# First stage of a decoder block: another order of loads, norms, rotary tables and latent projections

## The chip, the cores and the metric

One core of a Trainium2 chip runs the whole kernel. The time is the device time of one execution in microseconds (us); lower is better. The engines are TensorE (PE; its weight loads are listed apart as PEld), VectorE (DVE), ScalarE (ACT), GpSimd (POOL) and SyncE (SP), which here only issues transfers (DMA).

## What is computed

The reference is one decoder layer on x of 512 rows by 1024 columns, in float32:

```python
h = rmsnorm(x, g_mix)
z = h @ w_in      # [pool channels 512 | q latent 256 | kv latent 128 | rotary key 64 | gate A | gate B]
u_pool, c_q, c_kv, k_rope_in, gate_a, gate_b = split(z)
a  = pool_mixer(u_pool, ...)                 # windows 2/4/8/16, per-group maps
bm = mla_mixer(c_q, c_kv, k_rope_in, cos, sin, ...)   # norms of the latents, 8 heads, causal softmax
x = x + (sigmoid(gate_a) * a + sigmoid(gate_b) * bm) @ w_out
x = x + relu(rmsnorm(x, g_mlp) @ w_mlp_in)**2 @ w_mlp_out
out = rmsnorm(x, g_final)
```

cos and sin come from positions times inverse frequencies.

## The kernel before

Every float32 product is made of three passes on TensorE: an operand is split into a high part (a copy rounded to a narrower format, written by ScalarE) and a low part (operand minus high part, by VectorE), and high x high, low x high and high x low are added up in one PSUM bank. In the first stage the passes are called HH (high row, high weight), LH (low row, high weight) and HL (high row, low weight).

The first stage is what stands ahead of the gates. x comes as four tiles of 128 rows (`xs[0..3]`). For tile t, `square(t)` sums its squares on ScalarE and forms the reciprocal root (a small add on VectorE, a power on GpSimd), `scale_rows` multiplies the row by it and by the broadcast gain `g_bc` (two halves on VectorE, tile `n1h`), and `transpose_rows` turns it on TensorE through PSUM tiles `n1pt` (eight 128x128 transposes in two halves) and splits it into `h_hi` and `h_lo`.

The latent projection multiplies each tile by 448 columns of `w_in` (q latent, kv latent, rotary key). Its weights come as four chunks `C[0]` to `C[3]` of two row blocks each: `lat_hi(c)` casts a chunk's high part on ScalarE (`whi`), `lat_lo(c, engine)` makes its low part (`wlo`) on the engine named. `latents_mm(t, chunks, passes)` issues the matmuls, 24 for a tile, into that tile's PSUM tile `lat`. `latents_end(t)` norms the latents and turns the rotary key by the tables; `latents_t(t)` transposes the finished row `lrow` through PSUM tiles `lpt` and splits it.

The rotary tables (`ck`, `sk` and scaled copies) are made by a generator, `rotary_tables()`: some 15 small instructions on VectorE and two sines on ScalarE; each `next(rot)` issues a step of it. Then come the four pooling projections: `load_u(g)` loads and splits their weights, `pool_in(g)` does 24 matmuls of 512 columns into a PSUM tile `u`. The `lat` and `u` tiles share one pool of four banks (`psM`), so `u0` takes the bank of `lat` tile 0 and must wait until its last reader is done. Four raw buffers and four high and low buffers are shared by all weight chunks in turn.

Nothing is scheduled by cost here: all engines run their instructions in the order in which the code of this stage writes them (manual schedule), each engine for itself, and wait on each other by semaphores. SP issues the loads in the order written; eight can be on their way at a time, the ninth waits for the first. TensorE is kept busy at the start by `NWARM` matmuls on zeros (`warm`).

Of the kernel before, what the change touches and what calls it, by code (L numbers as in the profile page):

```python
# [11 lines left out]
F32 = mybir.dt.float32  # L12
# [7 lines left out]
P = 128  # L20
# [15 lines left out]
C_Q = PW  # L36
C_GA = PW + QL + KVL + DR
C_GB = C_GA + D
LAT = QL + KVL + DR
FFG = 8  # L40
NWARM = 4

COST = {"A": (0.165, 0.00083), "V": (0.155, 0.00104)}
UP_US, DOWN_US = 2.86, 2.78
# [4 lines left out]
def block_kernel(ctx: ExitStack, tc: tile.TileContext, x, positions, g_mix, w_in, b_gate,  # L49
                 pool_w, pool_scale, w_pool_proj, g_q, w_uq, g_kv, w_ukv, w_attn_proj,  # L50
                 w_out, g_mlp, w_mlp_in, w_mlp_out, g_final, inv_freq, inv_count, out):
    nc = tc.nc
# [43 lines left out]
    def load_chunk(srcs, cols, parts=False, own=None):  # L96

        n = nchunk[0]
        nchunk[0] += 1
        raw = wp.tile([P, 1024], F32, name=f"raw{n}", tag=f"raw{n % 4}", bufs=1)  # L100
        hi = (own or wp).tile([P, 1024], F32R, name=f"whi{n}", tag="whi", bufs=4)
        lo = (own or wp).tile([P, 1024], F32R, name=f"wlo{n}", tag="wlo", bufs=4)
        for view, src in srcs:
            nc.sync.dma_start(view(raw), src)
        if parts:
            return raw, hi, lo
        split(raw[:, :cols], hi[:, :cols], lo[:, :cols])
        return hi, lo
# [6 lines left out]
    w_in_v = w_in.rearrange("(k p) c -> p k c", p=P)  # L115
# [129 lines left out]
    with ExitStack() as pre:  # L245
# [14 lines left out]
        gl_bc = tb.tile([P, QL + KVL], F32, name="gl_bc")  # L260
        icnt = tb.tile([P, 16], F32, name="icnt")
        vrow = tb.tile([20, P], F32, name="vrow")
        nc.sync.dma_start(xs[0], x_v[0])
        nc.sync.dma_start(pos_i, positions.rearrange("(t p) -> p t", p=P))
        nc.sync.dma_start(frq, inv_freq.partition_broadcast(P))
        nc.sync.dma_start(g_bc, g_mix.partition_broadcast(P))
        nc.sync.dma_start(xs[1], x_v[1])
        lv = lambda t: t[:, :2 * LAT].rearrange("p (a b) -> p a b", a=2)
        lraw = [load_chunk([(lv, w_in_v[:, 2 * c:2 * c + 2, C_Q:C_Q + LAT])], 2 * LAT, True) for c in range(4)]
        lw = [(lv(hi), lv(lo)) for _, hi, lo in lraw]  # L270
        for t in (2, 3):
            nc.sync.dma_start(xs[t], x_v[t])
        nc.sync.dma_start(gl_bc[:, :QL], g_q.partition_broadcast(P))
        nc.sync.dma_start(gl_bc[:, QL:], g_kv.partition_broadcast(P))
        nc.sync.dma_start(vrow[:2 * KD, :], b_gate.rearrange("(k p) -> k p", p=P))
# [64 lines left out]
        lat_ps = {}  # L340

        def latents_mm(t, ks, passes):
# [5 lines left out]
            for k in ks:  # L348
                whi, wlo = lw[k // 2]
                for p in passes:  # L350
# [2 lines left out]
                    nc.tensor.matmul(ps[:, :LAT], h[:, k, tok], w[:, k % 2, :], start=len(done) == 1,  # L353
                                     stop=len(done) == 3 * KD)

        def latents_end(t):
            ps = lat_ps.pop(t)[0]
            junk = tmp1.tile([P, QL], F32, name=f"ljunk{t}", tag="ljunk", bufs=1)
            ms = small.tile([P, 2], F32, name=f"lms{t}", tag="lms")
            nc.scalar.activation(junk, ps[:, :QL], AF.Square, scale=1.0 / math.sqrt(QL), accum_out=ms[:, 0:1])  # L360
            nc.scalar.activation(junk[:, :KVL], ps[:, QL:QL + KVL], AF.Square,
                                 scale=1.0 / math.sqrt(KVL), accum_out=ms[:, 1:2])
            r = rstd_of(ms, 2, "l")
            row = tmp1.tile([P, 4, P], F32, name=f"lrow{t}", tag="lrow")
# [25 lines left out]
        def square(t):  # L390
            junk = tmp.tile([P, D], F32, name=f"n1junk{t}", tag="junk", bufs=1)
            ms = small.tile([P, 1], F32, name=f"n1ms{t}", tag="n1ms")
            nc.scalar.activation(junk, xs[t], AF.Square, scale=1.0 / math.sqrt(D), accum_out=ms)
            return rstd_of(ms, 1, "n1")

        def scale_rows(t, r):
            h = tmp.tile([P, D], F32, name=f"n1h{t}", tag="hrow")
            for c in range(2):
                cs = slice(c * 512, (c + 1) * 512)
                nc.vector.scalar_tensor_tensor(out=h[:, cs], in0=xs[t][:, cs], scalar=r, in1=g_bc[:, cs],  # L400
                                               op0=ALU.mult, op1=ALU.mult)
            return h

        def lat_hi(c):
            raw, hi, _ = lraw[c]
            nc.scalar.copy(hi[:, :2 * LAT], raw[:, :2 * LAT])

        def lat_lo(c, eng):
            raw, hi, lo = (t[:, :2 * LAT] for t in lraw[c])
            eng.tensor_tensor(out=lo, in0=raw, in1=f32(hi), op=ALU.subtract)  # L410


        def load_u(g):
            W["u", g] = chunk(w_in_v[:, :, g * P:(g + 1) * P], KD, P)
# [99 lines left out]
        rot = rotary_tables()  # L514
        C = [(2 * c, 2 * c + 1) for c in range(4)]
        HH, LH, HL = (0,), (1,), (2,)
        next(rot)
        r0 = square(0)
        next(rot)
        h0 = scale_rows(0, r0)  # L520
        r1 = square(1)
        next(rot)
        transpose_rows(h0, 0, h_hi, h_lo, psT, "n1")
        next(rot)
        lat_hi(0)
        latents_mm(0, C[0], HH)
        h1 = scale_rows(1, r1)
        lat_lo(0, nc.vector)
        lat_hi(1)
        lat_lo(1, nc.gpsimd)  # L530
        latents_mm(0, C[0], LH)
        latents_mm(0, C[1], HH)
        lat_hi(2)
        transpose_rows(h1, 1, h_hi, h_lo, psT, "n1")
        latents_mm(0, C[1], LH)
        latents_mm(0, C[0], HL)
        lat_hi(3)
        lat_lo(3, nc.gpsimd)
        lat_lo(2, nc.vector)
        latents_mm(0, C[2], HH + LH)  # L540
        latents_mm(1, C[0] + C[1], HH)
        latents_mm(0, C[1], HL)
        r2 = square(2)
        latents_mm(1, C[0], LH + HL)
        latents_mm(0, C[3], HH + LH)
        latents_mm(0, C[2], HL)
        next(rot)
        r3 = square(3)
        h2 = scale_rows(2, r2)
        latents_mm(0, C[3], HL)  # L550
        latents_mm(1, C[1], LH + HL)
        next(rot)
        transpose_rows(h2, 2, h_hi, h_lo, psT, "n1")
        h3 = scale_rows(3, r3)
        for _ in rot:
            pass
        latents_mm(1, C[2] + C[3], HH + LH + HL)
        latents_end(0)
        transpose_rows(h3, 3, h_hi, h_lo, psT, "n1")
        latents_mm(2, C[0] + C[1], HH + LH + HL)  # L560
        latents_end(1)
        latents_mm(2, C[2] + C[3], HH + LH + HL)
        latents_t(0)
        latents_mm(3, C[0] + C[1], HH + LH + HL)
        load_u(0)
        latents_end(2)
        latents_t(1)
        latents_mm(3, C[2] + C[3], HH + LH + HL)
        load_u(1)
        latents_end(3)  # L570
        pv = psT.tile([P, 20], F32, name="pv", tag="T")
        nc.tensor.transpose(pv, vrow, ident[:20, :20])
        nc.vector.tensor_copy(vec, pv)
        nrm.close()
        tmp2 = pool(mixer, "tmp2", bufs=2)
        pool_in(0)
        latents_t(2)
        nc.sync.dma_start(praw, pool_w.rearrange("g c d -> c g d"))
        load_u(2)
        pool_in(1)  # L580
        latents_t(3)
        pool_diff(0)
        load_u(3)
        pool_in(2)
        pool_diff(1)
        load_a(0)
# [898 lines left out]
```

## Time and profile before

| | |
|---|---|
| median of three runs | 684.94 us (684.65 to 686.38) |
| the profiled execution | 685.97 us, of which its span 684.2 us |
| mean granted TensorE clock | 0.991 of full speed (2.4 GHz) |
| TensorE busy | 663.0 us (97%) |
| VectorE, ScalarE, GpSimd busy | 516.0, 376.5, 83.2 us |

The span runs from the first to the last instruction of the program. A busy share over the whole span hides stages with different limits; the first 20 us look unlike the rest. The granted clock is the share of full speed that TensorE was given in a stretch: 1.00 is 2.4 GHz and 0.50 is 1.2 GHz; before the first recorded change it reads 1.00.

### The profile page before, as it was taken

The numbers are of one execution on the slowest core, as the hardware profiler recorded it, in microseconds if no ns is written. First come the engines' busy times: TensorE is split into PE (matmuls) and PEld (weight loads), VectorE is DVE, ScalarE is ACT, GpSimd is POOL, SyncE is SP. The second block draws the span as 40 slices with busy tenths as digits, with TensorE's granted clock in tenths as the row PEclk, the third lists the DMA queues.
The fourth block names the chain that finished last, engine by engine and source line by source line (L and its number), as shares of the span: only waits on it lengthen the run. The fifth ranks groups of instructions, "written<-read, shape, count | busy, mean of one in ns | idle before, by whom it ended". The sixth has DMA issues, their size and how long they took to land.

```text
span 684.2 us, 9775 instructions
## 1 busy us (share of the span) xinstructions
PE 663.0 (97%) x3681; PEld 570.0 (83%) x3681; DVE 516.0 (75%) x793; ACT 376.5 (55%) x613; POOL 83.2 (12%) x101
## 2 busy tenths in 40 slices
PE   6999999999999999999998999999999999999994
PEld 3888888888888888888888977899889988899883
DVE  5767852478788764564579989788987989799996
ACT  4545252446655544442267784488535874368735
POOL 2216600000000000000000212002200022001212
PEclk8999999999999999999999999999999999999998
DMA  7423354642221125747504679338973398444953
GB/s 274 139 62 94 95 152 129 174 128 63 69 69 47 47 93 186 224 130 233 166 0 125 174 170 238 96 123 183 215 188 122 95 215 174 135 154 140 231 92 124
DMA packets 87047, 95.24 MB, mean 139 GB/s; under 512 B 6468, under 2 KB 61528, under 8 KB 87000
## 3 DMA queue, kind: packets, MB, share of 16 engines
q1 hardware_dynamic: 78296, 77.84, 36.1%
q0 software_dynamic: 8704, 16.78, 14.5%
q8 instruction: 29, 0.48, 0.3%
q14 instruction: 18, 0.15, 0.1%
HBM read 88.31 MB, written 6.29 MB: 138 GB/s over the span
## 4 chain that ended last, share of the span: by engine, by line
PE 89%; DVE 5%; ACT 2%; issue 1%; DMA 1%; POOL 0%; SPq 0%; POOLq 0%; DVEq 0%; ACTq 0%
PE P L777 7%; PE P L778 7%; PE P L776 7%; PE b L826 6%; PE a L826 5%; PE c L826 3%; PE v L826 3%; PE u L421 3%; PE lat L353 3%; PE e L826 2%; PE wo L777 2%; PE ga L71 2%; PE gb L70 2%; PE ga L70 2%; PE wo L776 2%; PE ga L72 2%
## 5 line engine op out<-in xcount | busy, mean ns | idle before, releaser
L929 ACT CAST xhi<-r_X 128x1024 fp32r<-128x1024 f32 x84 | 88.1, 1051 | 68.8 <-PE P L778 25.7
L932 DVE TENSOR_TENSOR xlo<-r_X,xhi 128x1024 fp32r<-128x1024 f32 x84 | 102.5, 1222 | 20.8 <-ACT xhi L929 20.3
L777 PE MATMUL P<-xlo,rhi 128*128 128x512 f32 (+1 forms) x228 | 89.5, 392 | 1.6 <-DVE xlo L932 1.5
L778 PE MATMUL P<-xhi,rlo 128*128 128x512 f32 (+1 forms) x228 | 89.1, 391 | 0.0
L776 PE MATMUL P<-xhi,rhi 128*128 128x512 f32 (+1 forms) x228 | 89.1, 391 | 0.0
L65 ACT CAST whi<-raw 128x1024 fp32r<-128x1024 f32 x45 | 46.7, 1050 | 45.4 <-PE bm L71 17.2
L66 DVE TENSOR_TENSOR wlo<-raw,whi 128x1024 fp32r<-128x1024 f32 x45 | 55.3, 1234 | 18.7 <-ACT whi L65 17.5
L777 PEld LDWEIGHTS P<-xlo,rhi 128*128 128x128 f32 x228 | 42.7, 187 | 12.7 <-DVE xlo L932 2.9
L776 PEld LDWEIGHTS P<-xhi,rhi 128*128 128x128 f32 x228 | 42.7, 187 | 10.0
L778 PEld LDWEIGHTS P<-xhi,rlo 128*128 128x128 f32 x228 | 42.7, 187 | 10.0
L915 POOL DMA_DIRECT2D r_X<-in_w_mlp_out x24 | 29.1, 1210 | 120.9 <-DVE xlo L932 116.6
L940 DVE TENSOR_TENSOR r_X<-r_X,r_X 128x1024 f32<-128x1024 f32 x32 | 39.1, 1223 | 5.0 <-DMA r_X<-in_w_mlp_in 4.5
L1081 DVE TENSOR_TENSOR rlo<-F,rhi 128x512 fp32r<-128x512 f32 x56 | 37.6, 687 | 6.9 <-ACT rhi L1078 6.8
L1078 ACT CAST rhi<-F 128x512 fp32r<-128x512 f32 x56 | 33.3, 620 | 1.0 <-DVE F L1087 0.5
L1122 DVE TENSOR_TENSOR xa<-xa,P 128x512 f32<-128x512 f32 (+1 forms) x53 | 33.0, 672 | 0.7 <-PE P L778 0.7
L665 ACT ACTIVATE p<-s,nm 128x128 f32<-128x128 f32 (+3 forms) x32 | 16.9, 528 | 19.9 <-DVE nm L662 19.4
L915 POOL DMA_DIRECT2D r_T<-in_w_mlp_out x8 | 9.7, 1213 | 145.3 <-ACT rhi L1078 49.5
L826 PE MATMUL a<-mb_hi,xhi 128*128 128x256 f32 x96 | 27.0, 281 | 0.0
L826 PE MATMUL a<-mb_hi,xlo 128*128 128x256 f32 x96 | 27.0, 281 | 0.0
L826 PE MATMUL a<-mb_lo,xhi 128*128 128x256 f32 x96 | 27.0, 281 | 0.0
L70 PE MATMUL gb<-h_hi,whi 128*128 128x512 f32 x64 | 26.4, 412 | 0.0
L71 PE MATMUL gb<-h_lo,whi 128*128 128x512 f32 x64 | 25.6, 400 | 0.0
(297 smaller groups left out, 1923.9 us busy)
## 6 DMA issues: line engine op xcount, KB each, us to landing
r_X<-in_w_mlp_in SPq DMA_DIRECT2D x32, 512.0 KB, 4.6
r_X<-in_w_mlp_out POOLq DMA_DIRECT2D x24, 512.0 KB, 6.5
raw<-in_w_in SPq DMA_DIRECT2D x20, 512.0 KB, 4.0
r<-in_w_mlp_out SPq DMA_DIRECT2D x16, 512.0 KB, 6.2
raw<-in_w_attn_proj SPq DMA_DIRECT2D x8, 512.0 KB, 3.5
raw<-in_w_out SPq DMA_DIRECT2D x8, 512.0 KB, 4.9
r_X<-in_w_mlp_out SPq DMA_DIRECT2D x8, 512.0 KB, 4.0
r_T<-in_w_mlp_out SPq DMA_DIRECT2D x8, 512.0 KB, 4.0
```

Source lines behind the costliest of these rows:

```text
L65: nc.scalar.copy(hi, src)
L66: (lo_eng or nc.vector).tensor_tensor(out=lo, in0=src, in1=f32(hi), op=ALU.subtract)
L70: nc.tensor.matmul(acc, whi, ahi, start=first, stop=False)
L71: nc.tensor.matmul(acc, whi, alo, start=False, stop=False)
L776: nc.tensor.matmul(acc, a_hi, w_hi, start=first, stop=False, skip_group_check=again)
L777: nc.tensor.matmul(acc, a_hi, w_lo, start=False, stop=False, skip_group_check=again)
L778: nc.tensor.matmul(acc, a_lo, w_hi, start=False, stop=last, skip_group_check=again)
L826: nc.tensor.matmul(acc[:, j, :], u[:, k, js], b[:, k, :], start=fresh and j + k + n == 0, stop=j == 1 and k == 3 and n == 2, skip_group_ch ...
L915: op = Op("G", ADD_US, lambda: nc.gpsimd.dma_start(buf.tile.rearrange("p (a b) -> p a b", a=a), src, accum_op=ALU.add), needs, rank_now[0])
L929: nc.scalar.copy(hi, buf.tile)
L932: lo_op = use(vec_op(1024, lambda: nc.vector.tensor_tensor(out=pb.tile[1], in0=buf.tile, in1=f32(pb.tile[0]), op=SUB), [hi_op], k), buf)
L940: return use(vec_op(1024, lambda: nc.vector.tensor_tensor(out=O.tile, in0=A.tile, in1=Bb.tile, op=op), needs, rank_now[0]), *{A, Bb, O})
```

## The change

The loads are issued in another order; the steps of the rotary tables move behind the fourth tile's scaling; all four low parts of the latent weights are made on VectorE; `latents_end` is cut in two, so that the second half (`latents_row`) is issued one tile later, with four row buffers instead of two; the latent transposes move behind the first two pooling projections; the matmuls of the latent projection come in another order; and there are three warm-up matmuls instead of four.

```diff
-NWARM = 4
+NWARM = 3
...
         nc.sync.dma_start(xs[0], x_v[0])
+        nc.sync.dma_start(g_bc, g_mix.partition_broadcast(P))
+        load_lat(0)
+        nc.sync.dma_start(xs[1], x_v[1])
+        for c in (1, 2):
+            load_lat(c)
+        nc.sync.dma_start(xs[2], x_v[2])
+        load_lat(3)
+        lw = [(lv(hi), lv(lo)) for _, hi, lo in lraw]
+        nc.sync.dma_start(xs[3], x_v[3])
         nc.sync.dma_start(pos_i, positions.rearrange("(t p) -> p t", p=P))
         nc.sync.dma_start(frq, inv_freq.partition_broadcast(P))
-        nc.sync.dma_start(g_bc, g_mix.partition_broadcast(P))
-        nc.sync.dma_start(xs[1], x_v[1])
...
-            r = rstd_of(ms, 2, "l")
-            row = tmp1.tile([P, 4, P], F32, name=f"lrow{t}", tag="lrow")
+            lat_r[t] = rstd_of(ms, 2, "l")
+
+        def latents_row(t):
+            ps, r = lat_ps.pop(t)[0], lat_r.pop(t)
+            row = tmp1.tile([P, 4, P], F32, name=f"lrow{t}", tag="lrow", bufs=4)
...
-        next(rot)
         r0 = square(0)
-        next(rot)
         h0 = scale_rows(0, r0)
+        lat_hi(0)
+        transpose_rows(h0, 0, h_hi, h_lo, psT, "n1")
         r1 = square(1)
-        next(rot)
-        transpose_rows(h0, 0, h_hi, h_lo, psT, "n1")
-        next(rot)
-        lat_hi(0)
-        latents_mm(0, C[0], HH)
+        latents_mm(0, C[0], HH + LH)
+        lat_hi(1)
         h1 = scale_rows(1, r1)
         lat_lo(0, nc.vector)
-        lat_hi(1)
-        lat_lo(1, nc.gpsimd)
...
-        lat_lo(3, nc.gpsimd)
...
+        latents_mm(1, C[2], HH + LH)
         transpose_rows(h2, 2, h_hi, h_lo, psT, "n1")
+        lat_lo(3, nc.vector)
+        for t in range(2):
+            latents_mm(t, C[2], HL)
+            latents_mm(t, C[3], HH + LH)
         h3 = scale_rows(3, r3)
+        for _ in range(4):
+            next(rot)
+        for t in range(2):
+            latents_mm(t, C[3], HL)
+        latents_mm(2, C[0], HH + LH + HL)
+        transpose_rows(h3, 3, h_hi, h_lo, psT, "n1")
         for _ in rot:
             pass
...
         latents_end(1)
-        latents_mm(2, C[2] + C[3], HH + LH + HL)
-        latents_t(0)
-        latents_mm(3, C[0] + C[1], HH + LH + HL)
+        latents_row(0)
+        latents_mm(3, C[0], HH + LH + HL)
         load_u(0)
...
         pool_in(0)
+        latents_t(0)
+        latents_t(1)
+        load_u(3)
+        nc.sync.dma_start(praw, pool_w.rearrange("g c d -> c g d"))
+        pool_in(1)
         latents_t(2)
```

SP's queue at the start of the program, before; `x_115` to `x_118` are the four x tiles, `raw_...` with 2x448 the latent weight chunks, `pos_i` and `frq` positions and frequencies:

```order
L263 DMA x_115<-in_x 128x1024
L264 DMA pos_i<-in_positions 128x4x1
L265 DMA frq<-inv_freq 128x32
L266 DMA g_bc<-in_g_mix 128x1024
L267 DMA x_116<-in_x 128x1024
L104 DMA raw_128<-in_w_in 128x2x448
L104 DMA raw_132<-in_w_in 128x2x448
```

and now:

```order
L269 DMA x_115<-in_x 128x1024
L270 DMA g_bc<-in_g_mix 128x1024
L104 DMA raw_125<-in_w_in 128x2x448
L272 DMA x_116<-in_x 128x1024
L104 DMA raw_130<-in_w_in 128x2x448
L104 DMA raw_134<-in_w_in 128x2x448
L275 DMA x_117<-in_x 128x1024
L104 DMA raw_139<-in_w_in 128x2x448
L278 DMA x_118<-in_x 128x1024
L279 DMA pos_i<-in_positions 128x4x1
L280 DMA frq<-inv_freq 128x32
```

Positions and frequencies moved from the second and third place to behind the last x tile, and the first weight chunk to ahead of the second x tile.

VectorE from its fourth instruction on, before; `n1v` is the small add of a norm, `ang` and `kk` belong to the rotary tables:

```order
L293 CAST pos_f<-pos_i 128x4
L296 TENSOR_SCALAR ang<-frq,pos_f 128x32 x4
L88 TENSOR_SCALAR n1v<-n1ms_186 128x1
L314 TENSOR_SCALAR kk<-ang 128x128
L316 TENSOR_SCALAR kk<-kk 128x128
L400 SCALAR_TENSOR_TENSOR n1h_195<-x_115,n1r,g_bc 128x512 x2
L88 TENSOR_SCALAR n1v<-n1ms_199 128x1
L319 SCALAR_TENSOR_TENSOR ang<-kk,ang 128x128 x2
L66 TENSOR_TENSOR h_lo<-n1pt_0_207,h_hi 128x4x128
```

and now:

```order
L88 TENSOR_SCALAR n1v<-n1ms_178 128x1
L413 SCALAR_TENSOR_TENSOR n1h_184<-x_115,n1r,g_bc 128x512 x2
L66 TENSOR_TENSOR h_lo<-n1pt_0_188,h_hi 128x4x128
L66 TENSOR_TENSOR h_lo<-n1pt_1_195,h_hi 128x4x128
L88 TENSOR_SCALAR n1v<-n1ms_203 128x1
L413 SCALAR_TENSOR_TENSOR n1h_215<-x_116,n1r,g_bc 128x512 x2
L423 TENSOR_TENSOR wlo_127<-raw_125,whi_126 128x896
L66 TENSOR_TENSOR h_lo<-n1pt_0_224,h_hi 128x4x128
```

The table instructions no longer stand among the norms; the norm's add comes first.

TensorE's first rows, before; `lat_224` is the first tile's projection, `n1pt_0` and `n1pt_1` the two halves of a tile's transposes:

```order
L513 MATMUL warm<-wz 128x512 x4
L143 MATMUL n1pt_0_207<-ident,n1h_195 128x128 x4
L143 MATMUL n1pt_1_214<-ident,n1h_195 128x128 x4
L353 MATMUL lat_224<-whi_129,h_hi 128x448 x2
L353 MATMUL lat_224<-whi_129,h_lo 128x448 x2
L353 MATMUL lat_224<-whi_133,h_hi 128x448 x2
L143 MATMUL n1pt_0_238<-ident,n1h_227 128x128 x4
```

and now:

```order
L526 MATMUL warm<-wz 128x512 x3
L143 MATMUL n1pt_0_188<-ident,n1h_184 128x128 x4
L143 MATMUL n1pt_1_195<-ident,n1h_184 128x128 x4
L361 MATMUL lat_209<-whi_126,h_hi 128x448
L361 MATMUL lat_209<-whi_126,h_lo 128x448
L361 MATMUL lat_209<-whi_126,h_hi 128x448
L361 MATMUL lat_209<-whi_126,h_lo 128x448
L361 MATMUL lat_209<-whi_131,h_hi 128x448
```

A high and a low row now alternate, and four matmuls on the second chunk, not two, stand ahead of the second tile's transposes.

## Rows read from the trace of the kernel before

**Rows 1.** The page: TensorE's busy tenths in 40 slices of the span.

```profile
PE   6999999999999999999998999999999999999994
```

**Rows 2.** Windows: length, busy us of each engine, granted clock, DMA share, GB/s.

```profile
7.00:13.40 6.40, 2.54 (x13) 1.34 (x12) 4.15 (x13) 3.54 (x6) 1.11 (x2) 1.00 1.04 401
13.40:20.30 6.90, 6.00 (x21) 5.02 (x20) 6.51 (x7) 4.09 (x7) 3.24 (x2) 0.51 0.58 192
20.30:52.50 32.20, 32.16 (x165) 27.66 (x164) 22.08 (x66) 14.20 (x40) 6.83 (x9) 1.00 0.35 97
...
53.00:350.00 297.00, 297.00 (x1447) 247.04 (x1447) 192.47 (x353) 138.67 (x263) 27.56 (x41) 1.00 0.40 121
```

**Rows 3.** Chain that ended last, in order of time: start, us, what.

```profile
2.66 7.11 DMA x<-in_x
9.86 1.16 ACT n1junk L393 x2
...
13.37 3.26 DVE n1h L400 x2
...
25.13 0.87 PE n1pt L143 x8
...
29.61 4.96 PE lat L353 x24
...
46.27 0.44 PE lpt L385 x4
46.71 5.60 PE u L421 x24
```

**Rows 4.** Windows of the first loads; the last column is GB/s.

```profile
3.00:5.50 2.50, 2.50 (x4) 1.01 (x3) 0.17 (x1) 1.15 (x2) 0.00 (x0) 1.00 0.53 94
...
8.00:14.00 6.00, 2.45 (x12) 1.88 (x13) 4.30 (x10) 4.14 (x7) 0.82 (x2) 0.95 1.05 411
```

**Rows 5.** Timeline of the first 12 us: start, us, instruction, idle before it.

```profile
1.44 6.25 PE L513 MATMUL warm<-wz 128*128 128x512 f32 x8 [1.44 <-DVE hpi L283]
...
4.00 1.06 ACT L393 ACTIVATE n1junk<-x 128x1024 f32<-128x1024 f32 x1 [1.99 <-DMA x<-in_x]
...
6.29 0.68 DVE L296 TENSOR_SCALAR ang<-frq,pos_f 128x32 f32<-128x32 f32 x4 [1.54 <-DMA frq<-inv_freq]
...
8.63 1.41 DVE L400 SCALAR_TENSOR_TENSOR n1h<-x,n1r,g_bc 128x512 f32<-128x512 f32 x2 [1.14 <-DMA g_bc<-in_g_mix]
...
9.44 1.32 PE L143 MATMUL n1pt<-ident,n1h 128*128 128x128 f32 x8 [1.74 <-DVE n1h L400]
```

**Rows 6.** Groups by form, 0 to 20 us: busy us, mean ns of one.

```profile
L406 ACT CAST whi<-raw 128x896 fp32r<-128x896 f32 x4 | 3.6, 948 | 0.0
...
L66 DVE TENSOR_TENSOR h_lo<-n1pt,h_hi 128x512 fp32r<-128x512 f32 x4 | 2.7, 684 | 0.3 <-ACT h_hi L65 0.3
...
L65 ACT CAST h_hi<-n1pt 128x512 fp32r<-128x512 f32 x4 | 2.2, 582 | 2.8 <-PE n1pt L143 2.8
...
L319 DVE SCALAR_TENSOR_TENSOR ang<-kk,ang 128x128 f32<-128x128 f32 x4 | 1.1, 287 | 0.1
...
L90 POOL TENSOR_TENSOR n1r<-n1v,neghalf 128x1 f32<-128x1 f32 x2 | 1.1, 554 | 8.9 <-DVE n1v L88 8.9
```

**Rows 7.** Scalings (tile view: min/median/max ns), lows by engine (groups), one delayed add (timeline).

```profile
L400 DVE SCALAR_TENSOR_TENSOR n1h<-x,n1r,g_bc x8: 742/744/2584, 8.6 to 28.1; 128x512 f32<-128x512 f32 x8
...
L410 POOL TENSOR_TENSOR wlo<-raw,whi 128x896 fp32r<-128x896 f32 x2 | 5.1, 2560 | 5.2 <-ACT whi L406 5.2
...
L410 DVE TENSOR_TENSOR wlo<-raw,whi 128x896 fp32r<-128x896 f32 x2 | 2.2, 1080 | 0.0
...
20.46 1.80 DVE L314 TENSOR_SCALAR kk<-ang 128x128 f32<-128x128 f32 x1
```

**Rows 8.** Timeline: last table step on VectorE, last step of the first latent row.

```profile
29.33 0.29 DVE L327 SCALAR_TENSOR_TENSOR neg_abs<-ang 128x128 f32<-128x128 f32 x1
...
33.29 0.22 DVE L378 TENSOR_TENSOR lrow<-kt,kt 128x64 f32<-128x64 f32 x1
```

More of the change, by code (lines that the diff above doesn't have):

```diff
@@ L262, in block_kernel, with load_lat @@
         vrow = tb.tile([20, P], F32, name="vrow")
+        lv = lambda t: t[:, :2 * LAT].rearrange("p (a b) -> p a b", a=2)
+        lraw = []
+        def load_lat(c):
+            lraw.append(load_chunk([(lv, w_in_v[:, 2 * c:2 * c + 2, C_Q:C_Q + LAT])], 2 * LAT, True))
         nc.sync.dma_start(xs[0], x_v[0])
+        nc.sync.dma_start(g_bc, g_mix.partition_broadcast(P))
[7 more added lines that the diff above has]
+        nc.sync.dma_start(xs[3], x_v[3])
         nc.sync.dma_start(pos_i, positions.rearrange("(t p) -> p t", p=P))
         nc.sync.dma_start(frq, inv_freq.partition_broadcast(P))
-        nc.sync.dma_start(g_bc, g_mix.partition_broadcast(P))
-        nc.sync.dma_start(xs[1], x_v[1])
[L268 to L272, printed above, removed]
         nc.sync.dma_start(gl_bc[:, :QL], g_q.partition_broadcast(P))
@@ L354, in latents_mm @@
                                      stop=len(done) == 3 * KD)
+        lat_r = {}
         def latents_end(t):
-            ps = lat_ps.pop(t)[0]
+            ps = lat_ps[t][0]
             junk = tmp1.tile([P, QL], F32, name=f"ljunk{t}", tag="ljunk", bufs=1)
@@ L530, in block_kernel @@
-        lat_lo(1, nc.gpsimd)
-        latents_mm(0, C[0], LH)
-        latents_mm(0, C[1], HH)
+        latents_mm(0, C[1], HH + LH)
         lat_hi(2)
         transpose_rows(h1, 1, h_hi, h_lo, psT, "n1")
-        latents_mm(0, C[1], LH)
+        lat_lo(1, nc.vector)
         latents_mm(0, C[0], HL)
+        r2 = square(2)
+        latents_mm(0, C[2], HH + LH)
+        latents_mm(1, C[0], HH + LH + HL)
         lat_hi(3)
-        lat_lo(3, nc.gpsimd)
+        h2 = scale_rows(2, r2)
+        latents_mm(0, C[1], HL)
@@ L539, in block_kernel @@
+        latents_mm(1, C[1], HH + LH + HL)
         lat_lo(2, nc.vector)
[L540 to L547, printed above, removed]
         r3 = square(3)
[L549 to L552, printed above, removed]
+        latents_mm(1, C[2], HH + LH)
@@ L553, in block_kernel @@
         transpose_rows(h2, 2, h_hi, h_lo, psT, "n1")
+        lat_lo(3, nc.vector)
+        for t in range(2):
+            latents_mm(t, C[2], HL)
+            latents_mm(t, C[3], HH + LH)
         h3 = scale_rows(3, r3)
+        for _ in range(4):
[4 more added lines that the diff above has]
+        transpose_rows(h3, 3, h_hi, h_lo, psT, "n1")
         for _ in rot:
             pass
-        latents_mm(1, C[2] + C[3], HH + LH + HL)
@@ L558, in block_kernel @@
         latents_end(0)
-        transpose_rows(h3, 3, h_hi, h_lo, psT, "n1")
-        latents_mm(2, C[0] + C[1], HH + LH + HL)
+        latents_mm(2, C[1] + C[2] + C[3], HH + LH + HL)
         latents_end(1)
-        latents_mm(2, C[2] + C[3], HH + LH + HL)
-        latents_t(0)
-        latents_mm(3, C[0] + C[1], HH + LH + HL)
+        latents_row(0)
+        latents_mm(3, C[0], HH + LH + HL)
         load_u(0)
         latents_end(2)
-        latents_t(1)
-        latents_mm(3, C[2] + C[3], HH + LH + HL)
+        latents_row(1)
@@ L569, in block_kernel @@
+        latents_mm(3, C[1] + C[2] + C[3], HH + LH + HL)
         load_u(1)
         latents_end(3)
+        latents_row(2)
         pv = psT.tile([P, 20], F32, name="pv", tag="T")
@@ L573, in block_kernel @@
         nc.vector.tensor_copy(vec, pv)
+        latents_row(3)
+        load_u(2)
         nrm.close()
@@ L576, in block_kernel @@
         pool_in(0)
+        latents_t(0)
[3 more added lines that the diff above has]
+        pool_in(1)
         latents_t(2)
-        nc.sync.dma_start(praw, pool_w.rearrange("g c d -> c g d"))
-        load_u(2)
-        pool_in(1)
         latents_t(3)
         pool_diff(0)
-        load_u(3)
         pool_in(2)
```

## The prediction

> **What bounds the kernel now.** I read the page first. TensorE's line of busy tenths is full but for the first slice, one past the middle and the last [rows 1]. The stretches say the same more sharply: from 53 to 350 us TensorE has no gap at all [rows 2]. So whatever the first stage gives back or loses at its end should reach the end of the run, since nothing later has slack to swallow it; the instruction streams behind the fourth pooling projection are the same in both kernels.
>
> Next, the stage itself. From 7 to 13.4 us TensorE is busy for 2.54 of 6.40 us; then the granted clock reads 0.51 over 6.9 us, that is the 1.2 GHz level, and from 20.3 us on it is 1.00 (2.4 GHz) and TensorE works without a pause [rows 2]. What TensorE did before the clock fell was to idle for more than half of six microseconds; before it rose, it had been busy for most of the stretch (6.00 of 6.90 us). The chain of waits gives the causes in order: up to 9.77 us the second x tile's transfer, then VectorE scaling that tile (3.26 us for two halves, until 16.63), and only behind that mostly TensorE's own work [rows 3]. It is transfers and VectorE that hold the first 17 us, not matmuls.
>
> How much is lost? The third pooling projection (u2) starts at 46.71 + 5.60 + 0.44 = 52.75 us, and the first transpose at 9.44 [rows 3, 5]: 43.3 us. TensorE's own work between the two, at the full clock, is four tiles of eight transposes (0.87 each), four tiles of 24 latent matmuls (4.96 each), four groups of latent transposes (0.44), two projections (5.60) and about 0.2 for a small transpose [rows 3]: 3.5 + 19.8 + 1.8 + 11.2 + 0.2 = 36.5 us. So 6.8 us are idle time or half clock, and u2 is the place to compare: the work ahead of it is the same before and after, only ordered differently.
>
> **The change, part by part.**
>
> *Loads.* Today the small transfers of positions and frequencies stand second and third in SP's queue. While they pass (3 to 5.5 us) the engines move 94 GB/s; with only x rows and weights in the queue (8 to 14 us) they move 411 [rows 4]. The first x tile lands at 4.00 all the same, but g_mix, which the first scaling needs, lets VectorE start only at 8.63 [rows 5]. After the change g_mix is second. A 512 KB transfer takes 0.524/0.411 = 1.3 us, a weight chunk (448 KB) 1.1, so from 4.0 on my estimate is g_mix 5.3, chunk 0 6.4, x1 7.7, chunk 1 8.8, chunk 2 9.9, x2 11.2, chunk 3 12.3, x3 13.6. The bound on the bad side is that the broadcast of g_mix is slow by itself and lands at 8.5 as now. I take 5.3 to 5.8, since the small transfers fill just the stretch in which the rate is low. What is now last, positions and frequencies, lands behind x3, near 15; its first reader comes at 23.1 (below). The loads of the pooling weights wait for buffers, as now, and the buffers come free earlier.
>
> *First tile.* Square and its read-out 1.16 from 4.00 [rows 3, 5], then the sum on VectorE, no longer queued behind a multiply that waits for frequencies until 6.29 [rows 5], then the power on GpSimd 0.55 [rows 6], with some 0.2 for the small step and the handovers: 6.0. g_mix is there. Scaling takes 0.74 a half [rows 7], so the first transpose starts near 6.8 instead of 9.44. Three warm-up matmuls instead of four end between 6.1 (three quarters of 6.25 us) and 6.8, so they are not in the way; four would be [rows 5].
>
> *TensorE's remaining gaps.* By ScalarE's new order (chunk 0's high part 0.95 ahead of the tile's high halves, 0.58 each [rows 6]) the first latent matmul starts at 8.4: a gap of 0.4 behind the transposes. A chunk 0 that lands after 6.4 now holds up the high halves queued behind it on ScalarE, tenth for tenth. The tile's low half (0.68) opens the next at 9.1: 0.5. The four matmuls end at 9.7; ScalarE does square 1 (1.16) and chunk 1's high part (0.95) and lets the next four start at 10.8: 1.1. The second tile's transposes follow without a wait (VectorE has scaled its halves by 11.4 and 12.1), then chunk 0's low part (1.08 on VectorE [rows 7]) ends at 13.2: 0.6. From there TensorE has ready operands, but for about 0.3 at chunk 3's low part near 21.5. Together 2.9, and 0.3 for handovers: 3.2 us.
>
> *Lows on VectorE.* Two of four move from GpSimd, where one takes 2.56, to VectorE, 1.08 each: 2.2 us more on the engine that leads the chain. Against it stands what GpSimd's lows did to VectorE: of eight scalings the median is 0.744, but the one beside the first GpSimd low took 2.584, and a 0.23 us add beside the second took 1.80 [rows 7]. That is 1.8 + 1.6 = 3.4 us given back for 2.2 spent. VectorE's list from 12.1 is then four lows (4.3), four low halves (2.7), four scalings (2.9) and 1.1 for sums and one wait on GpSimd: the fourth tile is scaled at 23.1. TensorE, from 13.2, has 46 matmuls at 0.207, eight transposes and the 0.3 ahead of that tile's transposes: 23.9. VectorE leads by 0.8.
>
> The Trainium skill (SBUF — State Buffer, Who interferes with whom) has the rule behind these rows: a VectorE instruction with two SBUF inputs and a GpSimd instruction that reads SBUF exclude each other, and the later one stands still; the stretched rows agree. Its page Perfetto Trace Analysis (Optimizing Scalar/DVE Operations) speaks against the move: a saturated VectorE may be relieved by giving work to GpSimd, though it doubts this for these two. By that advice alone the move would cost the 2.2 us; by the rows it gains 1.2.
>
> *Rotary tables and latent rows.* About 4.1 us of tables (seven steps of 0.29 [rows 6], four multiplies in 0.68 [rows 5], some 1.4 of small ones) go behind the fourth scaling and cost TensorE nothing as long as it has other tiles' matmuls: it then has 42 of them. What is late next is the first latent row, which needs the tables and holds the bank that u0 wants. VectorE has 23.1 + 4.1 of tables + 1.4 for the last tile's low halves = 28.6 for the end of that part; in the trace the row's end follows it by 3.9 (29.62 to 33.51 [rows 8]): 32.5. TensorE asks at 6.8 + 3.2 + 3.5 + 19.8 + 0.2 = 33.5. One microsecond to spare. The latent transposes move behind u0 and u1 and cost the same 0.44 each; the rows they read are ready by 40.
>
> *Sum.* u2 starts at 6.8 + 36.5 + 3.2 = 46.5 instead of 52.75: 6.2 us earlier. I take 0.4 off for landings later than the estimate, since half a microsecond there shifts the first tile's high halves. Forecast: 5.8 us less. The profiled execution took 685.97 us (1.77 more than its span), so 680.2 by its own time; the median of the runs is 684.94, 1.03 lower, with 1.7 between the runs, and the trace cannot say whether that lies in this stage. I go half way: 679.7.
>
> **The rivals.** *The half clock stays.* TensorE still idles between 7 and 13.2 (2.6 of 6.2 us instead of 3.9 of 6.4), and has one warm-up less; if that still makes the clock fall at 13.4, it costs 1.7 us when it lasts half as long as now and 3.4 when it lasts as long, all of it now on the path: 681.4 to 683.1. For it: the gaps that are left; against: they are shorter than those ahead of the fall in the trace. The Trainium skill (TensorE: Matmul & The Clock Gate, What's actually happening) says that the throttled clock is the default and activity releases it; by that too the fall is possible with fewer warm-ups, and the trace shows the fall but not the point. Chance 0.20.
>
> *The loads come no earlier.* g_mix at 8.5 and all behind it 3.1 later: first transpose 9.3, and u2 at 9.3 + 36.5 + 3.2 = 49.0. The gain left is the chain's (no GpSimd lows, no tables ahead): 3.5 us with half of the allowance, so 682.0. With the half clock on top, under 1 us earlier: no change. Chance 0.14 for both, 0.04 of it the latter.
>
> *The table row becomes the bound.* This is the way to slower. If frequencies and positions, now last, land late, u0 waits for its bank: each microsecond past 24.1 (23.1 plus the spare 1.0) delays TensorE by one. It eats the gain at 30 us and is slower by over 0.3% at 32. Their queue has 4.5 MB ahead, 15 us by the rate above; it would take half that rate. Chance 0.03.
>
> The forecast keeps 0.63. The range runs from 678.3 (6.2 us off the median, and 0.4 if the first tile too lands sooner) to 682.9; it takes in late landings and most of the half-clock case. By over 0.3% (2.05 us, about what a measurement of this kernel tells from no change) faster: 0.63 + 0.15 + 0.09 = 0.87; within: 0.05 + 0.05 = 0.10; slower 0.03.
>
> **What would show it.** Right: the first transpose near 6.8, the second tile's near 11.6, the fourth scaling over by 23.1, u0 near 33.5 and u2 near 46.5, no 0.5 clock after 13.4, every scaling near 0.74. Wrong: a clock of 0.5 between 10 and 24; g_mix still released past 7; a wait of u0 on the latent row; or a gap behind 53 us that the trace of before does not have, through which the gain would be given back.

## The result and the profile after

The changed kernel took 681.1 us in the median of four runs (679.7 to 682.0) beside 685.3 for the kernel before on the same chip: ratio 0.9947, 95% interval 0.9929 to 0.9964. A later comparison gave 681.4 beside 684.6, 0.9951 (0.9933 to 0.9969). The forecast was 679.7 us with a range of 678.3 to 682.9, so the time lies in the range, 1.4 us above the number.

The profiled execution took 681.85 us, 680.1 of it its span: 4.1 us less than before. The chain of waits (start and duration in us) shows where TensorE stands:

```profile
1.65 6.32 DMA raw<-in_w_in
7.99 0.94 ACT whi L419
8.92 0.97 ACT h_hi L65 x2
9.89 1.05 ACT n1junk L406 x2
10.95 0.84 ACT whi L419
11.83 1.86 PE lat L361 x4
13.69 1.50 PE n1pt L143 x8
15.18 5.12 PE lat L361 x24
...
22.60 1.09 DVE wlo L423
23.74 2.33 PE lat L361 x10
26.07 0.87 PE n1pt L143 x8
26.94 8.67 PE lat L361 x42
35.61 0.17 PE pv L581
35.77 5.79 PE u L434 x24
...
48.90 11.19 PE u L434 x48
```

The chain no longer runs over x1 and VectorE's long scaling [rows 3] but over the load of weight chunk 0, then ScalarE. From 15.18 us on TensorE works without a pause, but for a quarter of a microsecond ahead of 23.74, where it waits for chunk 3's low part (the prediction had 0.3 there). The third pooling projection, u2, starts at 48.90 us instead of 52.75: 3.85 us earlier, nearly the whole of the 4.1 that the span lost. The stretches (us, then the stretch's length, busy time of PE, PEld, DVE, ACT, POOL, granted clock, DMA share, GB/s):

```profile
5.80:11.40 5.60, 2.70 (x13) 1.51 (x12) 2.86 (x5) 3.42 (x6) 0.52 (x2) 1.00 1.03 394
11.40:14.90 3.50, 3.07 (x11) 2.81 (x12) 2.42 (x3) 1.53 (x3) 0.36 (x1) 0.51 1.05 374
14.90:23.30 8.40, 8.40 (x47) 7.45 (x45) 6.78 (x11) 4.85 (x9) 1.09 (x2) 1.00 0.65 166
...
49.00:346.00 297.00, 297.00 (x1447) 247.03 (x1446) 190.56 (x355) 137.85 (x264) 26.78 (x40) 1.00 0.39 119
```

Set beside [rows 2], TensorE is full from 14.9 us instead of 20.3, and the stretch at the 1.2 GHz level is 3.5 us long instead of 6.9. It is still there. From 49 to 346 us TensorE has no gap, as before.

The first tile (timeline; in brackets the idle time ahead and what ended it) and the eight scalings as a group (duration min/median/max in ns):

```profile
6.66 1.41 DVE L413 SCALAR_TENSOR_TENSOR n1h<-x,n1r,g_bc 128x512 f32<-128x512 f32 x2 [1.17 <-DMA g_bc<-in_g_mix]
7.46 1.32 PE L143 MATMUL n1pt<-ident,n1h 128*128 128x128 f32 x8 [1.63 <-DVE n1h L413]
7.99 0.94 ACT L419 CAST whi<-raw 128x896 fp32r<-128x896 f32 x1 [2.68 <-DMA raw<-in_w_in]
...
L413 DVE SCALAR_TENSOR_TENSOR n1h<-x,n1r,g_bc x8: 744/746/752, 6.7 to 24.3; 128x512 f32<-128x512 f32 x8
```

The first transpose starts 2 us earlier than in [rows 5]; g_mix still ends the wait ahead of it, at 6.66 us where the prediction had 5.3 to 5.8. No scaling is stretched any more (2584 ns at the most in [rows 7]).

### The profile page after: what moved, and what is told of

It is laid out like the page before. It is cut to its first block, busy times and chain, and to the rows that moved or that the text cites. A ratio compares the mean times of both kernels' runs of the same rounds, so it can differ in the third digit from the quotient of the medians.

```text
span 680.1 us, 9767 instructions
## 1 busy us (share of the span) xinstructions
PE 660.2 (97%) x3679; PEld 568.4 (84%) x3679; DVE 512.7 (75%) x795; ACT 376.0 (55%) x613; POOL 77.7 (11%) x99
## 4 chain that ended last, share of the span: by engine, by line
PE 87%; DVE 5%; DMA 3%; ACT 2%; issue 1%; POOL 1%; SPq 0%; POOLq 0%; DVEq 0%; ACTq 0%
PE P L789 6%; PE P L790 6%; PE P L788 6%; PE b L838 5%; PE a L838 5%; PE u L434 3%; PE c L838 3%; PE v L838 3%; PE lat L361 3%; PE e L838 3%; PE wo L789 2%; PE gb L70 2%; PE ga L71 2%; PE ga L72 2%; PE wo L788 2%; PE ga L70 2%
## 5 line engine op out<-in xcount | busy, mean ns | idle before, releaser
L1090 ACT CAST rhi<-F 128x512 fp32r<-128x512 f32 x56 | 33.3, 620 | 1.3 <-DVE F L1099 0.8
```

## The experiments

Ratios are to the kernel before on the same chip. u2 is read from the chain of the run's own profile; 52.75 us before.

| run | what it is | median us | ratio (95%) | u2 |
|---|---|---|---|---|
| e5_after_again | changed kernel | 681.4 | 0.9951 (0.9933-0.9969) | 48.78 |
| e1_old_loads | loads undone | 684.7 | 1.0004 (0.9992-1.0016) | 52.07 |
| e2_gpsimd_lows | lows undone | 683.3 | 0.9985 (0.9971-0.9999) | 51.02 |
| e3_tables_early | tables undone | 684.6 | 1.0006 (0.9992-1.0019) | 52.40 |
| e12_transposes_early | latent transposes undone | 690.6 | 1.0100 (1.0081-1.0118) | 57.95 |
| e8_loads_alone | loads alone, on before | 693.1 | 1.0127 (1.0099-1.0155) | 59.99 |
| e10_lows_alone | lows alone, on before | 682.5 | 0.9972 (0.9958-0.9986) | 49.26 |
| e6_gain_plain | gain as plain rows | 681.7 | 0.9963 (0.9944-0.9981) | 47.63 |
| e7_gain_by_matmul | gain spread by TensorE | 682.5 | 0.9967 (0.9951-0.9983) | 50.64 |
| e9_hold_x1 | x1's load held | 682.8 | 0.9974 (0.9960-0.9987) | 50.68 |
| e4_fill | gaps filled | 681.9 | 0.9967 (0.9950-0.9984) | 48.37 |
| e11_no_warm | no warm-ups | 681.5 | 0.9961 (0.9949-0.9974) | 49.41 |

**The measure.** 

> The changed kernel itself, unaltered, as the measure for the runs beside it. My theory: 0.9947 of the kernel before, within 0.0015 (681 us), with the stretch of half clock from 11.4 us on again and the third pooling projection near 48.9 us. The rival, that the first comparison flattered it: 0.997 to 1.0.

 Measured 0.9951; half clock again, from about 11.2 us on, u2 at 48.78. The gain repeats.

**Loads undone.**

```diff
-        nc.sync.dma_start(g_bc, ...); load_lat(0); nc.sync.dma_start(xs[1], ...)
+        nc.sync.dma_start(pos_i, ...); nc.sync.dma_start(frq, ...)
+        nc.sync.dma_start(g_bc, ...); nc.sync.dma_start(xs[1], ...)
+        lraw = [load_chunk(...) for c in range(4)]
```

> The changed kernel with the loads alone in their old order (x0, positions, frequencies, g_mix, x1, the four weight chunks, x2, x3); all else as changed. My theory: the loads are about half of the gain. Chunk 0 lands near 10.9 us as in the trace of before instead of 8.0, g_mix near 8.6 instead of 6.7, so the first transpose starts near 9.3, the first latent matmul near 12.4 instead of 9.46, and the third pooling projection 2 to 2.9 us later: 683.6 us (682.8 to 684.6) beside 681.1 for the changed kernel. The rival, that the loads are hidden behind the norms and the gain comes from the lows, the tables and the clock: 681.1, within 0.6.

 Measured 1.0004: no gain is left at all. The chain:

```profile
3.14 7.51 DMA raw<-in_w_in
...
11.52 1.07 ACT h_hi L65 x2
...
14.51 1.86 PE lat L353 x4
```

Chunk 0 lands at 10.65 us. In the new order its cast stands on ScalarE ahead of the first tile's high halves, so they wait for it (11.52 instead of 8.92), and the second four matmuls start at 14.51 instead of 11.83. The cost is larger than I expected (some 3.6 us by the ratios, not 2.5), because the new order of ScalarE counts on an early chunk 0. Up to the second four matmuls that is 2.7 us. Behind them the half clock takes its share: in this execution it lasts from 8.7 to 18.9 us, 10.2 us instead of 3.4, and u2 is 3.2 us late. Over its twelve runs the mean granted clock is 0.988 to 0.991, over the changed kernel's ten 0.991 to 0.997.

**Lows undone.**

```diff
-        lat_lo(1, nc.vector)
+        lat_lo(1, nc.gpsimd)
...
-        lat_lo(3, nc.vector)
+        lat_lo(3, nc.gpsimd)
```

> The changed kernel with the low parts of chunks 1 and 3 made on GpSimd again; all else as changed. My theory: GpSimd's lows hold VectorE up by more than the 2.2 us that they spare it (one scaling or low half stretched to about 2.5 us beside each, 3.4 us together): slower by 1.2 us, 682.3 us (681.6 to 683.6), and a stretched VectorE instruction beside each GpSimd low. The rival, that GpSimd's lows are harmless and VectorE, which leads, is relieved: 1 to 2.2 us faster, 679 to 680.

 Measured 0.9985, 2.3 us of the gain lost (0.9985 against 0.9951), and u2 2.2 us later than in e5_after_again. VectorE and GpSimd at the place:

```profile
11.88 2.64 POOL L423 TENSOR_TENSOR wlo<-raw,whi 128x896 fp32r<-128x896 f32 x1
11.83 3.25 DVE L413 SCALAR_TENSOR_TENSOR n1h<-x,n1r,g_bc 128x512 f32<-128x512 f32 x2 [0.67 <-POOL n1r L90]
```

The second tile's two scalings take 3.25 us beside GpSimd's low instead of 1.42, with the rest of VectorE's work behind them; the first matmul behind that tile's transposes starts at 16.13 us, 1.2 later than in the changed kernel (14.94). The other microsecond at u2 goes with the half clock, which lasts 6.8 us in this execution (12.5 to 19.4) instead of 3.4. The expected stretch beside the second low did not come: VectorE stood idle there. That GpSimd's lows relieve VectorE is wrong here.

**Lows alone**, on the kernel before:

```diff
-        lat_lo(1, nc.gpsimd)
+        lat_lo(1, nc.vector)
...
-        lat_lo(3, nc.gpsimd)
         lat_lo(2, nc.vector)
+        lat_lo(3, nc.vector)
```

> The kernel before with one part of the change alone: the low parts of chunks 1 and 3 made on VectorE (chunk 3's behind chunk 2's). My theory: the scaling that took 2.58 us takes 0.74, the add of 1.80 takes 0.23, against 2.2 us more work; the second tile's transposes end 1.6 us earlier and the third pooling projection comes 0.9 us earlier: 683.7 us (683.0 to 684.4) beside 684.6. The rival, that VectorE leads and only gets more work: 1 us or more slower than before, 685.6.

 Measured 0.9972: 1.9 us faster, twice what I expected. The group of scalings, and the stretch that stood at half clock in [rows 2]:

```profile
L400 DVE SCALAR_TENSOR_TENSOR n1h<-x,n1r,g_bc x8: 743/746/752, 8.4 to 24.6; 128x512 f32<-128x512 f32 x8
...
13.40:20.30 6.90, 6.87 (x37) 5.70 (x36) 6.84 (x12) 5.09 (x9) 0.40 (x1) 1.00 0.87 283
```

No scaling is stretched; and in this execution the clock did not fall, so u2 (3.5 us earlier) shows more than the median. Its mean granted clock, 0.996, is reached by one other of the twelve runs; the rest have 0.990 to 0.994. What the scalings and the clock have to do with each other, this run does not tell.

**Tables undone.**

```diff
         latents_mm(1, C[0], HH + LH + HL)
         lat_hi(3)
+        for _ in range(4):
+            next(rot)
         h2 = scale_rows(2, r2)
...
+        for _ in rot:
+            pass
         h3 = scale_rows(3, r3)
-        for _ in range(4):
-            next(rot)
```

> The changed kernel with the rotary tables' steps put back ahead of the third and the fourth tile's scalings; loads and lows as changed. My theory: VectorE leads the chain up to the fourth scaling, which ends at 25.0 us with 1.1 us to spare ahead of the transposes that read it; 4.1 us of tables in front of it (and a wait for the sines) make TensorE wait about 3 us there: 684.1 us (683 to 685.5). The rival, that VectorE has enough idle time in this part (0.66 us ahead of each scaling) and the tables may stand anywhere: 681.1 to 681.7.

 Measured 1.0006, 3.8 us of the gain lost. In the chain the last scaling and the transposes that read it come 3.2 us later than in the changed kernel (29.22 against 26.07):

```profile
28.41 0.67 DVE n1h L413
...
29.22 0.64 PE n1pt L143 x4
```

**Latent transposes undone.**

```diff
         latents_row(0)
+        latents_t(0)
         latents_mm(3, C[0], HH + LH + HL)
...
         latents_row(1)
+        latents_t(1)
         latents_mm(3, C[1] + C[2] + C[3], HH + LH + HL)
...
         pool_in(0)
-        latents_t(0)
-        latents_t(1)
```

> The changed kernel with the latent transposes of the first two tiles put back ahead of the last tile's matmuls, right behind the rows that they read; the tables stay late. My theory: the move of these transposes, which I priced at nothing, is needed by the late tables: the first row is ready at 34.7 us and TensorE asks near 30.7, so it waits 4 us there: the first pooling projection near 39.7 instead of 35.7, 685.2 us (684.3 to 686). The rival, that the place of these transposes is of no account: 681.4, within 0.6.

 The direction was right, the size was half: 1.0100, u0 at 45.68 us. TensorE's rows with a wait:

```profile
32.89 0.82 PE L398 MATMUL lpt<-ident,lrow 128*128 128x128 f32 x3 [3.10 <-DVE lrow L380]
33.87 0.47 PE L398 MATMUL lpt<-ident,lrow 128*128 128x128 f32 x1 [0.16 <-DVE lrow L391]
39.07 0.59 PE L398 MATMUL lpt<-ident,lrow 128*128 128x128 f32 x3 [2.49 <-DVE lrow L380]
40.05 0.47 PE L398 MATMUL lpt<-ident,lrow 128*128 128x128 f32 x1 [0.39 <-DVE lrow L391]
```

I had counted the first stall and not the second. Tile 1's row stands on VectorE behind the low part of u0's weights, whose cast gets its buffer only when tile 3's first matmuls are done; those stand behind the stalled transposes. The clock fell twice on top, for 3.4 us each (from 33.0 and from 39.6 us).

**Loads alone**, on the kernel before, in the new order. 

> The kernel before with the new order of the loads alone; tables among the norms, lows on GpSimd, four warm-ups as before. My theory: the parts need one another. The first table step stands first in VectorE's list and now waits for positions and frequencies, which land last, near 16.5 us, so the first scaling starts near 17.8 instead of 8.6; what the loads gave TensorE then comes back in part, since all weights have landed: 6.5 us slower than before (4.5 to 9), 691 us. The rival, that the loads' gain stands by itself: 2 to 3 us faster than before, 682.

 Measured 1.0127, 8.5 us slower. VectorE's first row of the tables:

```profile
15.65 0.17 DVE L301 CAST pos_f<-pos_i 128x4 f32<-128x4 int32 x1 [14.24 <-DMA pos_i<-in_positions]
```

With the tables first in VectorE's list, positions at the queue's end hold the first scaling to 17.30 us. In this order the loads can move only with the tables; the new order with positions and frequencies left early was not run.

**The gain as plain rows.**

```diff
-        nc.sync.dma_start(g_bc, g_mix.partition_broadcast(P))
+        nc.sync.dma_start(g_bc, x_v[0])
```

> The changed kernel with the gain loaded as 128 different rows of x (512 KB, the same bytes into the same tile) in place of one row of 4 KB sent to all partitions; the norm is therefore scaled by other numbers, so the output is not the reference's. My theory: it is the broadcast itself that is slow (213 to 256 GB/s while it passed, 410 behind it). As plain rows it lands by 5.6 us instead of 6.7, chunk 0 near 6.8 instead of 8.0, the third pooling projection 1.1 us earlier: 680.0 us (679.4 to 680.6) beside 681.1. The rival, that any transfer in the first 7 us runs slowly, whatever its source: no landing moves by more than 0.3 us, 681.1 within 0.4.

 The theory fell. The first scaling is no longer held by the gain (6.04 us), but ScalarE gets chunk 0 at 7.68, only 0.2 to 0.3 earlier. The rate dips without a broadcast too, though less (344 and 285 GB/s from 4 to 6 us, where the changed kernel has 213 and 256):

```profile
5.00:6.00 1.00, 1.00 (x3) 0.33 (x1) 0.15 (x1) 0.18 (x2) 0.54 (x1) 1.00 0.91 285
...
7.68 0.94 ACT L419 CAST whi<-raw 128x896 fp32r<-128x896 f32 x1 [2.50 <-DMA raw<-in_w_in]
```

u2 comes 1.15 to 1.27 us earlier than in the changed kernel's two profiles (47.63), in an execution whose clock did not fall.

**The gain spread by TensorE.**

```diff
-        nc.sync.dma_start(g_bc, g_mix.partition_broadcast(P))
+        nc.sync.dma_start(grow, g_mix.rearrange("(o d) -> o d", o=1))
...
-NWARM = 3
+NWARM = 2
...
+        for c in range(2):
+            nc.tensor.matmul(g_ps[c], one_row, grow[:, c * 512:(c + 1) * 512], start=True, stop=True)
```

> The changed kernel with the gain loaded as one row of 4 KB on one partition and spread over the 128 partitions by two TensorE matmuls with a row of ones, into two PSUM tiles that the scalings read; two warm-ups instead of three. 508 KB leave the queue. My theory: chunk 0 lands near 6.7 us instead of 8.0, x1 near 8 instead of 9.3, the first scaling starts by 6.3 us and the third pooling projection 1.3 us earlier: 679.8 us (679.0 to 680.5) beside 681.1. The rival, that the chain is not led by the loads or that the two matmuls end after 7 us and hold the first scaling up: 681 to 682.

 The rival held: 0.9967. The two matmuls took 1.85 us each (the two warm-ups ahead of them 1.89, so this is the low clock), and each half of the first scaling waited for its own:

```profile
5.16 3.77 PE L530 MATMUL g_ps<-grow,one_row 1*128 1x512 f32 x4
...
7.33 0.75 DVE L415 SCALAR_TENSOR_TENSOR n1h<-x,n1r,g_ps 128x512 f32<-128x512 f32 x1 [1.91 <-PE g_ps L530]
8.97 0.75 DVE L415 SCALAR_TENSOR_TENSOR n1h<-x,n1r,g_ps 128x512 f32<-128x512 f32 x1 [0.89 <-PE g_ps L530]
```

Chunk 0 was there at 7.52 us: 508 KB fewer in the queue brought it 0.4 to 0.5 us, not 1.3.

**x1's load held.**

```diff
+        wz = tmp.tile([P, D], F32, name="wz", tag="late", bufs=1)
+        xs = [tmp.tile([P, D], F32, name=f"x{t}", tag="late" if t == 1 else "xt", ...) for t in range(NT)]
```

> The changed kernel with x1's load, and so all loads queued behind it, held until the warm-up matmuls are over (x1 takes the buffer whose zeros they read); only x0, the gain and chunk 0 are then on their way up to 5.8 us. The gain as plain rows brought chunk 0 from 7.92 to 7.68 us only, so the broadcast is not what made it late. My theory now: chunk 0 shares the transfer engines with the loads queued behind it. Without them it lands by 6.4 us, and x1 near 9.5; the third pooling projection moves by less than 0.5 us either way, since x1 then sets the second tile: 681.4 us within 0.8. The rival, that the rate is low between 4 and 6.5 us (223 to 229 GB/s) whatever is queued: chunk 0 lands at 7.0 or later, everything behind it 1 us later or more, 682.5 or above.

 The rival held for the landing: chunk 0 at 7.56 us, 0.4 earlier. SP issued chunk 1's load ahead of the held one, so that one still stood beside chunk 0's (SP's issues, and ScalarE's cast):

```profile
1.65 0.94 SPq L104 DMA_DIRECT2D raw<-in_w_in  x2
5.76 0.34 SPq L277 DMA_DIRECT2D x<-in_x  x1
...
7.56 0.94 ACT L422 CAST whi<-raw 128x896 fp32r<-128x896 f32 x1 [2.26 <-DMA raw<-in_w_in]
```

Chunk 0 without any load behind it was thus not run. The cost (u2 at 50.68, 1.8 to 1.9 us late) is x1's first: its square starts at 10.79 us and the second four matmuls at 12.81, 1.0 late. The rest goes with a half clock of 6.8 us (11.2 to 18.0) instead of 3.4.

**Gaps filled.**

```diff
+        def fill(n):
+            for _ in range(n):
+                nc.tensor.matmul(warm[:, :P], wz[:, :P], wz[:, :P], start=True, stop=True)
+        fill(4)
...
+        fill(4)
         latents_mm(0, C[0], HH + LH)
+        fill(3)
```

> The changed kernel with eleven more matmuls of 128 columns on zeros where TensorE idles: four behind the warm-ups, four behind the first tile's transposes, three behind the first four latent matmuls. They add work and no information. My theory: part of the miss of the forecast is the half clock from 11.4 to 14.8 us; if these make the clock stay up, TensorE's 3.07 us of work there take half, but VectorE leads behind it, so 0.9 us come back at the most: 680.2 (679.6 to 680.8), and the granted clock at 1.00 throughout. The rival, that the clock is not the cause, or that the filling stands in the way: 681.1 to 682.

 The clock stayed at 1.00:

```profile
11.40:14.90 3.50, 3.12 (x20) 2.30 (x19) 2.83 (x5) 2.68 (x5) 0.55 (x1) 1.00 1.04 373
```

u2 came 0.4 to 0.5 us earlier than in the changed kernel's two profiles, though this execution's chunk 0 landed 0.3 to 0.4 us later. The time shows nothing of it (0.9967, an interval that overlaps the changed kernel's). For the clock one profile proves little: it stayed up without any filling in those of e6_gain_plain and e12_transposes_early, whose TensorE does the same work up to 30 us. The nine runs say more: their mean granted clock is 0.995 to 0.997, where the changed kernel's ten runs spread from 0.991 to 0.997. That points to the filling, but as a mean over the whole span it does not say where the clock fell.

**No warm-ups** (`NWARM = 0`). 

> The changed kernel without any warm-up matmul, so that TensorE does nothing up to the first transpose at 7.3 us. My theory: TensorE runs at the 1.2 GHz level until it has worked for some time (the warm-ups take 1.9 us each at first, 0.86 once the clock is up), so the first two tiles' transposes and the first latent matmuls go at half speed to 15 us or beyond; the third pooling projection 1.5 to 2.5 us later than in the changed kernel: 683.2 us (682.4 to 684.2). The rival, that the clock matters little because VectorE and the loads lead: 681.4, within 0.6.

 The rival held: 0.9961. TensorE then runs the whole first part at half speed:

```profile
7.51 1.97 PE L143 MATMUL n1pt<-ident,n1h 128*128 128x128 f32 x8 [7.51 <-DVE n1h L413]
9.49 0.74 PE L361 MATMUL lat<-whi,h_hi 128*128 128x448 f32 x1
```

The first latent matmul takes 0.74 us here and 0.47 in the changed kernel, and full speed comes only near 16.4 us. Yet u2 comes at 49.41, only 0.5 to 0.6 us later than in the changed kernel's profiles, in which the clock fell: loads, ScalarE and VectorE set most of the pace.

## Why the forecast held, and where it was off

*Nothing later swallows it.* Right: u2 and the span moved by 3.85 and 4.1 us.

*Lows on VectorE.* Right, and undersized: I put the move at 1.2 us of gain; undone it costs 2.3, alone it gives 1.9. My sum weighed VectorE's work alone (3.4 less 2.2 us). The stretched scaling also stands in the second tile's path, and in the execution of e2_gpsimd_lows the half clock was longer. The prediction also sets both stretched rows of [rows 7] beside a rule for instructions with two inputs; the one of 1.80 us reads a single tile (`kk<-ang`), so only the scaling speaks for that rule.

*Tables behind the norms, latent rows.* Right. The row ends at 34.68 us and u0 starts at 35.77, without a wait; the spare 1 us is 1.1. The prediction priced both steps at nothing as long as they are covered; e3_tables_early and e12_transposes_early show what the covers are worth (3.8 and 10 us).

*Loads.* This is the term that was mis-sized. I counted 1.3 us for each 512 KB from 4.0 us on, one transfer behind another: chunk 0 at 6.4. Measured 7.96, and with it the first latent matmul at 9.46 instead of 8.4 and the second four at 11.83 instead of 10.8: 1.0 us. Two things were wrong in it. The first is the rate, which is not 411 GB/s there:

```profile
4.00:5.00 1.00, 1.00 (x3) 0.53 (x2) 0.00 (x0) 0.84 (x1) 0.00 (x0) 1.00 0.67 213
5.00:6.00 1.00, 0.83 (x2) 0.00 (x1) 0.15 (x1) 0.30 (x2) 0.42 (x1) 1.00 0.81 256
6.00:7.00 1.00, 0.00 (x0) 0.00 (x0) 0.34 (x1) 0.00 (x0) 0.13 (x1) 1.00 0.99 346
7.00:8.00 1.00, 0.54 (x4) 0.42 (x4) 1.00 (x2) 0.01 (x1) 0.00 (x0) 1.00 1.06 410
```

I had put the dip of before (94 GB/s) down to the small transfers; it is shallower without them, not gone. The 1.51 MB of x0, the gain and chunk 0 had been moved by 7.1 us (45 + 283 + 336 + 213 + 256 + 346 KB up to 7 us). The second is that chunk 0 was released only 0.9 us after that, when the engines had moved about 1.87 MB. Half of that lag a transfer shows even by itself: in the kernel before, x0's 0.52 MB had passed by 3.5 us, the engines then moved next to nothing (8 GB/s), and ScalarE was released at 4.00:

```profile
3.00:3.50 0.50, 0.50 (x2) 0.19 (x1) 0.00 (x0) 0.00 (x0) 0.00 (x0) 1.00 0.84 215
3.50:4.00 0.50, 0.50 (x2) 0.15 (x1) 0.00 (x0) 0.00 (x1) 0.00 (x0) 1.00 0.30 8
```

And loads queued behind are moved ahead of its end. e7_gain_by_matmul shows it best: x0, the row and chunk 0 are 0.99 MB, but 1.59 MB had been moved when chunk 0 was released at 7.52. What makes the rate dip, and how lag and rate share the 1.5 us, stays open: without the broadcast 1.51 MB had passed by 6.4 us, and chunk 0 still came at 7.66. Neither the broadcast (0.3 us), nor the bytes ahead (0.4 to 0.5 us for 508 KB), nor x1 and what stands behind chunk 1 (0.4 us) makes up the 1.5 by itself; they were not taken away together.

*The half clock.* It had 0.20 as a rival, because the gaps left were shorter than those ahead of the fall before, and it was a sign named for being wrong. It came, from 11.42 to 14.84 us. Its price can be read from executions of nearly the same work in which the clock did not fall. ScalarE takes chunk 0 up at these times in e5_after_again, e4_fill and e11_no_warm (7.99 and 7.68 in the changed kernel and e6_gain_plain, above):

```profile
7.92 0.94 ACT whi L419
...
8.33 0.94 ACT whi L419
...
8.02 0.94 ACT L419 CAST whi<-raw 128x896 fp32r<-128x896 f32 x1 [2.73 <-DMA raw<-in_w_in]
```

From there to u2 it is 40.9 us in the two profiles of the changed kernel, 40.0 in e4_fill and e6_gain_plain, where the clock stayed up, and 41.4 in e11_no_warm, at half speed up to 16.4 us. The fall thus cost 0.9 us, and my price for such a stretch, 1.7 us, was too high. I had put all of it on the path; but with the clock up, the chain of e4_fill and e6_gain_plain runs over VectorE (the second tile's scaling and chunk 0's low part), which hides a part, as the expectation of e4_fill had it.

So u2, 2.4 us later than I said (0.4 of which was allowed for), is late by 1.5 for the loads and 0.9 for the clock; neither turned the forecast. What stands between chunk 0 and u2 I had at 46.5 - 6.4 = 40.1 us, and 40.0 was measured with the clock up. That is closer than its parts, and partly luck: TensorE works without a pause from 6.3 us behind chunk 0's landing there, not 6.8, and from then on takes 33.7 us to u2, not 33.3.

*The parts do not add up.* I summed them one by one. Undone singly, loads, lows and tables cost 3.6, 2.3 and 3.8 us, where all of them together gave 3.4 to 3.6; alone, the loads cost 8.5. Each part holds the cover of another. Where the half clock lasts longer, as with loads or lows undone, a part's price takes that in; whether the edit made it longer there is not shown. The new order of the latent matmuls and the four warm-ups were not put back singly. No version here is faster than the changed kernel.

## What to carry to other kernels

A load moved to the queue's end takes every instruction that waits for it, and all behind that on its engine, with it; move the reader first. Undo parts one by one before you credit them: a sum of single gains is wrong where one part is the cover of the next. Do not count a landing in the first microseconds from the rate that the engines reach later, nor from the bytes ahead alone: here chunk 0 was released 0.9 us after those had passed. Before a microsecond is credited to an edit, compare the granted clock of the two executions.

## What the runs showed of the hardware beyond that

The granted-clock column reads 1.00 ahead of the first recorded change, whatever TensorE does: in e11_no_warm it reads so over the first latent matmuls, which take 0.74 us and then 0.58, where those behind 16.5 us take 0.36. The three warm-ups took 4.39 us together in the changed kernel's profile and 5.49 in that of e6_gain_plain. So executions differ in when full speed comes, and durations of matmuls tell it where the column does not.

Runs of one kernel also differ far behind the change. TensorE's only wait between 440 and 670 us, in the profiled executions before and after (after's row: us in total, times, longest):

```profile
PE b L838 <- DVE xlo L944: 0.9, 1, 0.9
```

e5_after_again, the same kernel, does not have it and has a span 1.4 us shorter, with u2 only 0.1 earlier. A wait of a microsecond for a late weight in the last stage is thus part of the spread of the runs, and a reason to read a change in the first stage at u2 as well as in the time.
